# Layer 0's side work kept in emitted order on its engines, gates loaded a group ahead, and v's transposes moved between two groups' items

## The chip, the cores and the metric

One core of one Trainium2 chip. The metric is the device time of one execution in microseconds (us), as the median of several runs of the same program; a smaller number is better. The five engines that work here are TensorE (PE), VectorE (DVE), ScalarE (ACT), GpSimd (POOL) and SyncE (SP, which only issues DMAs in this kernel). Each takes its instructions in one fixed order, and an instruction that waits holds up all that stand behind it on its engine.

## The reference

Two layers of a bidirectional encoder over 512 tokens with 16 learned meta tokens ahead of them (528 rows, width 2048). Layer 0 is grouped-query softmax attention (16 query heads, 8 key/value heads of 128), layer 1 gated linear attention. The change touches layer 0 alone:

```python
y = rmsnorm(h, pre_norm[0])
proj = y @ w_in                                    # q 2048, k 1024, v 1024, gate 2048
q, k, v, gate = jnp.split(proj, [...], axis=-1)
q = apply_axial_rope(rmsnorm(q, q_norm), ...)      # per head of 128
k = apply_axial_rope(rmsnorm(k, k_norm), ...)
o = softmax(q @ k.T * 128 ** -0.5) @ v             # two query heads share one k and v
y = (o * silu(gate)) @ w_out
h = h + rmsnorm(y, post_norm[0])
```

## The kernel before, in words

All matmuls are fp32, done as three products of halves: an activation tile `src` is split into a high part (a cast on ACT, L131) and a rest (a subtraction on DVE, L132), a weight tile likewise (`whi`, `wlo`), and `hi*hi + lo*hi + hi*lo` is summed in PSUM. The normalised input lies as `uh` and `ul` for the whole layer.

**The first part (about 121 to 291 us).** The projections for gates 3 to 12 and for v of seven groups are made two tiles at a time by `seven` (L216), which forms sums of weight quarters on DVE (L233), runs seven products on PE (L240 to L242), copies or adds them up (`y`, ACT L270 and the like, DVE L249), and stores the tiles to DRAM as `g_d` (POOL queue, L569). Beside it runs `first_group` (L524), which normalises and rotates k, q, q of group 0: a square on ACT (L528), sums over the partitions on PE (`ssq`, L536), scale and shift on DVE (L538), `rotate` (L310: four DMAs qs<-qw on POOL's queue, then three multiplies and adds on POOL, L314 to L316), the inverse root on ACT, and the multiply qw*sq on DVE (L543).

**The groups (about 291 to 775 us).** One group per key/value head, some 60.5 us each. In the stretch of group g, PE runs three projections for group g+1 (`project`, L158: k, q, q; tiles `pp`) as its bulk, and between their matmuls stand those of group g's attention: nine items, one each 3.3 us. An item is `softmax`: scores s on PE (L682 to L684), the maximum on DVE (mx, L687), the exponential on ACT (pn, L690; its row sum is inverted on DVE, rs, L696); half a slot later `transposed`: four transposes into pT and one into pTm on PE (L702, L704), read by ACT (ph, L706; pmt, L708) and DVE (pl, L707; pmt, L709), and later the product with v (`weighted`). The PSUM tile s has one buffer. The PSUM pool `ps_t` has two, and pT, pTm and the tiles vps and vpm of v's transposes take them in turn.

**The side work of a group.**

- `rope` (L318) of the three projected tiles, each at three delays after the projection: two partition sums ssq (L327) with sq on DVE (L330), then the inverse root on ACT (L135, L136) and the multiply qw*f (DVE, L334).
- `values(g+1)` (L601): the tile vt is loaded from g_d by SP (L606), at 13.0 it is transposed (PE vps, L611, and vpm, L618), and from there vh is made on ACT (L614), vl on DVE (L615), and the small vm (L620 to L622).
- `stored_gates` (L648) for two gates: load gr<-g_d on POOL's queue (L652), gr times rrow on DVE (L656), the sigmoid as three ACT passes (L139 to L141), gs times gr on POOL (L670); then `inverse` (L637), a load of the stored reciprocals r_d into the same gr buffer, `divided` on POOL (L641, L642), the product with the held o_sb (L663), and the store og_d (L664).

**What sets the order.** The program is emitted by a model of time, `Clock` (L39): each PE matmul of a projection advances it by a cost, and generators and delayed functions are emitted when the model reaches their due time (`yield 8.0`, `clk.after(13.0, ...)`). Then the builder's scheduler orders every engine's queue by priority and by when inputs are ready in its own simulation: it may float an instruction whose inputs are ready early ahead of others emitted before it. So the gates of before do not stand where their generator emits them: gr has two buffers, and a gate's load and its multiplies stand as soon as a buffer is free, about one gate each half group, from 292 us on and up to a group ahead of the stretch for which they are due. `tc.high_priority` raises a stretch of emission; `tc.keep_in_program_order`, which the change brings in as `pin`, ties an instruction behind the one emitted before it on its engine, without a wait.

Of the kernel before, what the change touches and what calls it, by code (L numbers as in the profile page):

```python
# [13 lines left out]
AF = mybir.ActivationFunctionType  # L14
ALU = mybir.AluOpType
# [4 lines left out]
P = 128  # L20
D = 2048
KT = D // P
SEQ = 512
META = 16
T = SEQ + META
# [6 lines left out]
KV = 8  # L32
# [50 lines left out]
def hybrid_encoder(  # L83
# [5 lines left out]
    nc = tc.nc  # L89
    V, A, G, PE = nc.vector, nc.scalar, nc.gpsimd, nc.tensor  # L90
    clk = Clock()

    def pool(stack, name, bufs=1, **kw):
        return stack.enter_context(tc.tile_pool(name=name, bufs=bufs, reuse_waits="tile", **kw))
# [8 lines left out]
    og_d = scratch.tile([KT, P, T], F32, name="og_d")  # L103
    h1_d = scratch.tile([4, P, D], F32, name="h1_d")
    g_d = scratch.tile([21, P, T], F32, name="g_d")
    r_d = scratch.tile([KV, 2, T], F32, name="r_d")
# [189 lines left out]
    rrow = c0.tile([P, T], F32, name="rrow")  # L296
    erow = c0.tile([P, T], F32, name="erow")
# [20 lines left out]
    def rope(qw, sq, outs, steps):  # L318
        rotate(qw, wk.tile([P, T], F32, tag="qs", name="qs"))
        sh = wk.tile([P, T], F32R, tag="sh", name="sh", bufs=1)  # L320
        sl = wk.tile([P, T], F32R, tag="sl", name="sl", bufs=1)
        split(sh, sl, sq)
        f = sq

        def sums(a, b):
            ps = ps_p.tile([P, 512], F32, tag="pp", name="ssq")[:, :b - a]
            PE.matmul(ps, ones_r, sh[:, a:b], start=True, stop=False)  # L327
            PE.matmul(ps, ones_r, sl[:, a:b], start=False, stop=True)
            with tc.high_priority(AHEAD):
                V.scalar_tensor_tensor(f[:, a:b], ps, 1.0 / P, erow[:, a:b], op0=ALU.mult, op1=ALU.add)  # L330

        def late():
            rsqrt_inplace(f)
            V.tensor_tensor(qw, qw, f, op=ALU.mult)  # L334
            for hi, lo, a, b in outs:
                split(hi, lo, qw[:, a:b])
        for step, part in zip(steps, HALVES):
            clk.after(step, lambda part=part: sums(*part))
        clk.after(steps[2], late)
# [11 lines left out]
    vt = c0.tile([P, T], F32, name="vt")  # L351
# [50 lines left out]
    for i, (si, off) in enumerate(((0, 0), (1, 0), (1, P))):  # L402
        for j, (a, b) in enumerate(HALVES):
            n = 2 * i + j
            if n < 3:
                ps = ps_p.tile([P, 512], F32, tag="pp", name="pp")
            else:
                ps = ps_g.tile([P, 512], F32, name=f"g{n}")
            ps = ps[:, :b - a]
# [114 lines left out]
    def first_group():  # L524

        for qw, w in zip(qws, (KN, QN, QN)):
            sq = fr.tile([P, T], F32, tag="sq", name="sq")
            A.activation(sq, qw, AF.Square)  # L528
            A.activation(qw, qw, AF.Copy, scale=col(w))
            for a, b in HALVES:  # L530
                parts = fr.tile([P, 2, HALF], F32R, tag="qs", name="shl")
                sh, sl = parts[:, 0], parts[:, 1]
                split(sh, sl, sq[:, a:b])
                yield 5.6
                ps = ps_t.tile([P, 512], F32, tag="t", name="ssq")[:, :HALF]
                PE.matmul(ps, ones_r, sh, start=True, stop=False)  # L536
                PE.matmul(ps, ones_r, sl, start=False, stop=True)
                V.scalar_tensor_tensor(sq[:, a:b], ps, 1.0 / P, erow[:, a:b], op0=ALU.mult, op1=ALU.add)  # L538
                yield 0.2
            rotate(qw, fr.tile([P, T], F32, tag="qs", name="qs"))  # L540
            rsqrt_inplace(sq)
            yield 9.4
            V.tensor_tensor(qw, qw, sq, op=ALU.mult)  # L543
            yield 0.4

    def y_tiles():
        return [yp.tile([P, T], F32, tag=f"y{i}", name=f"y{i}") for i in range(2)]
# [2 lines left out]
    for h in range(3):  # L550
        y = yp.tile([P, T], F32, tag=f"y{h % 2}", name="y")
# [49 lines left out]
    def values(g):  # L601
        vh = wa.tile([P, 4, P], F32R, tag="vh", name="vh")
        vl = wa.tile([P, 4, P], F32R, tag="vl", name="vl")
        vm = vm_bufs[g % 2]
        if g:
            clk.after(4.0, lambda: nc.sync.dma_start(out=vt, in_=g_d[13 + g]))  # L606

        def late():
            ps = ps_t.tile([P, 512], F32, tag="t", name="vps")
            for t in range(4):  # L610
                PE.transpose(ps[:, t * P:(t + 1) * P], vt[:, t * P:(t + 1) * P], ident)  # L611
            for t in range(4):
                pst = ps[:, t * P:(t + 1) * P]
                A.activation(vh[:, t, :], pst, AF.Copy, scale=rcol[:, t:t + 1])  # L614
                V.scalar_tensor_tensor(vl[:, t, :], pst, rcol[:, t:t + 1], vh[:, t, :].bitcast(F32),  # L615
                                       op0=ALU.mult, op1=ALU.subtract)
            pm = ps_t.tile([P, 512], F32, tag="t", name="vpm")[:META, :P]
            PE.transpose(pm, vt[:, SEQ:T], ident)  # L618
            rm = rcol[:META, 4:5]
            A.activation(vm[0:META], pm, AF.Copy, scale=rm)  # L620
            A.activation(vm[64:64 + META], pm, AF.Copy, scale=rm)
            V.scalar_tensor_tensor(vm[32:32 + META], pm, rm, vm[0:META].bitcast(F32),  # L622
                                   op0=ALU.mult, op1=ALU.subtract)
        clk.after(13.0 if g else 2.0, late)
        return vh, vl, vm

    def qkv(g):
        qk, outs = qks[g % 2]
        vv = values(g)
        for i, c in enumerate((2048 + g * P, 2 * g * P, (2 * g + 1) * P)):  # L630
            qw, sq, evac = take(col(KN if i == 0 else QN))
            project(w_in0, c, HALVES, evac)
            rope(qw, sq, outs[i], (4.0, 8.8, 9.8))
        return qk, vv

    def inverse(h, rb):
        nc.gpsimd.dma_start(out=rb, in_=r_d[h // 2, h % 2:h % 2 + 1, :].broadcast_to([P, T]))  # L637

    def divided(gs, rb):
        by = gs[:, :SEQ].rearrange("p (t q) -> p t q", t=4)  # L640
        G.tensor_tensor(by, by, rb[:, :SEQ].rearrange("p (q t) -> p t q", t=4), op=ALU.mult)  # L641
        G.tensor_tensor(gs[:, SEQ:], gs[:, SEQ:], rb[:, SEQ:], op=ALU.mult)  # L642

    def inverses(g, rs, a):
# [2 lines left out]

    def stored_gates(hs, held):  # L648

        grs = [wa.tile([P, T], F32, tag="gr", name="gr") for _ in hs]  # L650
        for gr, h in zip(grs, hs):
            nc.gpsimd.dma_start(out=gr, in_=g_d[h])  # L652
        yield 8.0
        gss = []
        for gr, h in zip(grs, hs):
            V.tensor_tensor(gr, gr, rrow, op=ALU.mult)  # L656
            gss.append(silu(gr))
            inverse(h, gr)
            yield 5.0
        for gr, gs, h in zip(grs, gss, hs):  # L660
            divided(gs, gr)
            og = held[h % 2]
            G.tensor_tensor(og, og, gs, op=ALU.mult)  # L663
            nc.gpsimd.dma_start(out=og_d[h], in_=og)  # L664
            yield 3.0

    def silu(gr):
        gs = wa.tile([P, T], F32, tag="gs", name="gs", bufs=2)
        sigmoid(gs, gr)
        G.tensor_tensor(gs, gs, gr, op=ALU.mult)  # L670
        return gs

    def gate(h, last_k=None):
# [876 lines left out]
```

## Time and profile before

| | us |
|---|---|
| median of 3 runs | 1800.95 (1796.97 to 1801.56) |
| profiled execution, its own time | 1799.52 |
| its span | 1797.5 |
| PE busy | 1746.3 (97%) |
| DVE, ACT, POOL busy | 1141.4, 1005.9, 383.2 |
| first part with `seven` | about 121 to 291 |
| eight groups | about 291 to 775 |

The span is the time from the first to the last instruction that the profiler recorded; 2.0 us of the execution lie around it. Idle time in front of an instruction is put down to what ended it (the "releaser"). An engine that is 97% busy has few gaps, and what a change of order can bring is the gaps that it closes; so the views that list PE's waits come first, and then the rows that show why the releaser was late.

### The profile page before, as it was taken

The numbers are of one execution on the slowest core, as the hardware profiler recorded it, in microseconds if no ns is written. First come the engines' busy times: TensorE is split into PE (matmuls) and PEld (weight loads), VectorE is DVE, ScalarE is ACT, GpSimd is POOL, SyncE is SP. The second block draws the span as 40 slices with busy tenths as digits, with TensorE's granted clock in tenths as the row PEclk, the third lists the DMA queues.
The fourth block names the chain that finished last, engine by engine and source line by source line (L and its number), as shares of the span: only waits on it lengthen the run. The fifth ranks groups of instructions, "written<-read, shape, count | busy, mean of one in ns | idle before, by whom it ended". The sixth has DMA issues, their size and how long they took to land. (4 is left out here: it accounts for less than half of the span.)

```text
span 1797.5 us, 31585 instructions
## 1 busy us (share of the span) xinstructions
PE 1746.3 (97%) x12427; PEld 1636.9 (91%) x12427; DVE 1141.4 (63%) x1791; ACT 1005.9 (56%) x2056; POOL 383.2 (21%) x492
## 2 busy tenths in 40 slices
PE   8999999999998999999999999999999999999998
PEld 8999999988898889999999899988898989888886
DVE  5867776565656556696757866667585765764223
ACT  5634446576666665654447544468685765853221
POOL 3103202544555453242131101110000100000000
PEclk9999999999999999999999999999999999999999
DMA  8444434334333334264485444343242332344333
GB/s 258 140 121 125 125 119 137 96 85 101 106 92 96 94 93 119 86 202 129 129 242 177 119 130 119 95 133 105 79 116 74 110 95 81 100 150 175 94 94 129
DMA packets 272387, 218.80 MB, mean 122 GB/s; under 512 B 13196, under 2 KB 243280, under 8 KB 271712
## 3 DMA queue, kind: packets, MB, share of 16 engines
q1 hardware_dynamic: 253200, 157.41, 30.9%
q0 software_dynamic: 19040, 59.40, 10.5%
q8 instruction: 97, 1.59, 0.4%
q14 instruction: 50, 0.41, 0.1%
HBM read 176.83 MB, written 33.44 MB: 117 GB/s over the span
## 5 line engine op out<-in xcount | busy, mean ns | idle before, releaser
L154 PE MATMUL pp<-uh,whi 128*128 128x264 f32 (+1 forms) x1872 | 585.4, 313 | 0.7 <-POOL whi L383 0.5
L156 PE MATMUL pp<-uh,wlo 128*128 128x264 f32 (+1 forms) x1872 | 576.1, 308 | 1.5 <-DVE wlo L132 1.2
L155 PE MATMUL pp<-ul,whi 128*128 128x264 f32 (+1 forms) x1872 | 575.7, 308 | 0.8 <-DVE ul L445 0.8
L132 DVE TENSOR_TENSOR wlo<-wraw,whi 128x1024 fp32r<-128x1024 f32 (+1 forms) x226 | 276.2, 1223 | 234.4 <-ACT whi L131 230.5
L131 ACT CAST whi<-wraw 128x1024 fp32r<-128x1024 f32 (+1 forms) x226 | 235.4, 1042 | 256.4 <-PE f L1462 83.4
L156 PEld LDWEIGHTS pp<-uh,wlo 128*128 128x128 f32 x1872 | 353.3, 189 | 18.9 <-DVE wlo L132 1.7
L154 PEld LDWEIGHTS pp<-uh,whi 128*128 128x128 f32 x1872 | 353.3, 189 | 17.4 <-POOL whi L383 0.8
L155 PEld LDWEIGHTS pp<-ul,whi 128*128 128x128 f32 x1872 | 353.7, 189 | 14.7 <-DVE ul L445 1.4
L131 ACT CAST whi<-x 128x1024 fp32r<-128x1024 f32 x72 | 75.5, 1049 | 110.0 <-PE pp L241 55.1
L132 DVE TENSOR_TENSOR wlo<-x,whi 128x1024 fp32r<-128x1024 f32 x72 | 89.9, 1254 | 43.5 <-ACT whi L131 43.5
L240 PE MATMUL px<-uh,whi 128*128 128x264 f32 x288 | 82.7, 287 | 1.9 <-ACT whi L131 1.9
L242 PE MATMUL px<-uh,wlo 128*128 128x264 f32 x288 | 82.8, 288 | 0.7 <-DVE wlo L132 0.7
L241 PE MATMUL px<-ul,whi 128*128 128x264 f32 x288 | 82.2, 285 | 0.0
L687 DVE TENSOR_REDUCE mx<-s 128x1 f32<-128x528 f32 (+1 forms) x72 | 50.6, 703 | 39.4 <-PE s L684 38.7
L1462 PE MATMUL f<-whi,ul 128*128 128x512 f32 x192 | 75.6, 394 | 0.0
L1460 PE MATMUL f<-whi,uh 128*128 128x512 f32 x192 | 75.5, 393 | 0.0
L1461 PE MATMUL f<-wlo,uh 128*128 128x512 f32 x192 | 75.3, 392 | 0.0
L690 ACT ACTIVATE pn<-s,mx 128x528 f32<-128x528 f32 (+1 forms) x72 | 50.1, 696 | 40.5 <-DVE mx L687 40.3
L313 POOL DMA_DIRECT2D qs<-qw x96 | 47.8, 504 | 93.4 <-issue 33.6
L707 DVE TENSOR_TENSOR pl<-pT,ph 128x512 fp32r<-128x512 f32 (+1 forms) x80 | 47.6, 595 | 24.1 <-ACT ph L706 23.4
L240 PE MATMUL pp<-t0h,whi 128*128 128x264 f32 x192 | 55.6, 289 | 3.7 <-ACT y L270 3.7
L240 PEld LDWEIGHTS px<-uh,whi 128*128 128x128 f32 x288 | 54.7, 190 | 2.1 <-ACT whi L131 2.1
(488 smaller groups left out, 4433.4 us busy)
## 6 DMA issues: line engine op xcount, KB each, us to landing
wraw<-in_gla_w_in_dram SPq DMA_DIRECT2D x82, 512.0 KB, 4.0
wraw<-in_attn_w_in_dram SPq DMA_DIRECT2D x75, 512.0 KB, 4.4
wraw<-in_gla_w_out_dram SPq DMA_DIRECT2D x32, 512.0 KB, 3.9
wraw<-in_attn_w_out_dram SPq DMA_DIRECT2D x23, 512.0 KB, 4.3
x<-in_attn_w_in_dram SPq DMA_DIRECT2D x19, 512.0 KB, 4.3
x<-in_gla_w_in_dram SPq DMA_DIRECT2D x14, 512.0 KB, 4.6
qs<-qw POOLq DMA_DIRECT2D x96, 66.0 KB, 4.5
g_d<-y POOLq DMA_DIRECT2D x20, 264.0 KB, 2.4
```

The source lines that it names most:

```text
L131: A.copy(hi, src)
L132: V.tensor_tensor(lo, src, hi.bitcast(F32), op=ALU.subtract)
L154: PE.matmul(ps, wh, uh[:, k, a:b], start=first, stop=False)
L155: PE.matmul(ps, wh, ul[:, k, a:b], start=False, stop=False)
L156: PE.matmul(ps, wl, uh[:, k, a:b], start=False, stop=last)
L240: PE.matmul(ps, w[0][:, k], bh[:, k], start=k == 0 and not more, stop=False, skip_group_check=more)
L241: PE.matmul(ps, w[0][:, k], bl[:, k], start=False, stop=False, skip_group_check=more)
L242: PE.matmul(ps, w[1][:, k], bh[:, k], start=False, stop=k == KH - 1, skip_group_check=more)
L687: V.reduce_max(mx, s, axis=AX.XY, negate=True)
L1460: PE.matmul(ps, uh[:, k, ts], wh[:, kk], start=(k == 0), stop=False)
L1461: PE.matmul(ps, uh[:, k, ts], wl[:, kk], start=False, stop=False)
L1462: PE.matmul(ps, ul[:, k, ts], wh[:, kk], start=False, stop=(k == KT - 1))
```

## The change

No instruction of the computation is added or removed. Four things are done:

1. **Pins.** The Square, the scale-and-shift and the multiply of `first_group`, the gate loads, gr*rrow, gs*gr, the load of the reciprocals, `divided`'s first multiply and the load of vt keep their place in emitted order on their engine. `divided`'s 16-wide tail is not pinned.
2. **Gates a group ahead.** The two gate tiles of the next group are loaded at the end of `stored_gates` of this one; the steps of `stored_gates` have new delays, the second gate begins 2.2 after the first instead of 5.0.
3. **v's transposes** for groups 2 to 7 are due at 5.0 instead of 13.0 (group 1 stays at 13.0, group 0 at 2.0), and vt is loaded 1.0 after the transposes that read it last. vt's new index, 14 + g, is the next group's tile, as before.
4. **New delays** in `first_group` and `rope`.

```diff
--- before.py
+++ after.py
@@ -89,6 +89,7 @@
     nc = tc.nc
     V, A, G, PE = nc.vector, nc.scalar, nc.gpsimd, nc.tensor
     clk = Clock()
+    pin = tc.keep_in_program_order
 
     def pool(stack, name, bufs=1, **kw):
         return stack.enter_context(tc.tile_pool(name=name, bufs=bufs, reuse_waits="tile", **kw))
@@ -525,23 +526,23 @@
 
         for qw, w in zip(qws, (KN, QN, QN)):
             sq = fr.tile([P, T], F32, tag="sq", name="sq")
-            A.activation(sq, qw, AF.Square)
+            pin(A.activation(sq, qw, AF.Square))
             A.activation(qw, qw, AF.Copy, scale=col(w))
             for a, b in HALVES:
                 parts = fr.tile([P, 2, HALF], F32R, tag="qs", name="shl")
                 sh, sl = parts[:, 0], parts[:, 1]
                 split(sh, sl, sq[:, a:b])
-                yield 5.6
+                yield 6.0
                 ps = ps_t.tile([P, 512], F32, tag="t", name="ssq")[:, :HALF]
                 PE.matmul(ps, ones_r, sh, start=True, stop=False)
                 PE.matmul(ps, ones_r, sl, start=False, stop=True)
-                V.scalar_tensor_tensor(sq[:, a:b], ps, 1.0 / P, erow[:, a:b], op0=ALU.mult, op1=ALU.add)
-                yield 0.2
+                pin(V.scalar_tensor_tensor(sq[:, a:b], ps, 1.0 / P, erow[:, a:b], op0=ALU.mult, op1=ALU.add))
+                yield 1.0
             rotate(qw, fr.tile([P, T], F32, tag="qs", name="qs"))
             rsqrt_inplace(sq)
-            yield 9.4
-            V.tensor_tensor(qw, qw, sq, op=ALU.mult)
-            yield 0.4
+            yield 13.0
+            pin(V.tensor_tensor(qw, qw, sq, op=ALU.mult))
+            yield 5.0
 
     def y_tiles():
         return [yp.tile([P, T], F32, tag=f"y{i}", name=f"y{i}") for i in range(2)]
@@ -602,8 +603,9 @@
         vh = wa.tile([P, 4, P], F32R, tag="vh", name="vh")
         vl = wa.tile([P, 4, P], F32R, tag="vl", name="vl")
         vm = vm_bufs[g % 2]
-        if g:
-            clk.after(4.0, lambda: nc.sync.dma_start(out=vt, in_=g_d[13 + g]))
+
+        def load():
+            pin(nc.sync.dma_start(out=vt, in_=g_d[14 + g]))
 
         def late():
             ps = ps_t.tile([P, 512], F32, tag="t", name="vps")
@@ -621,7 +623,9 @@
             A.activation(vm[64:64 + META], pm, AF.Copy, scale=rm)
             V.scalar_tensor_tensor(vm[32:32 + META], pm, rm, vm[0:META].bitcast(F32),
                                    op0=ALU.mult, op1=ALU.subtract)
-        clk.after(13.0 if g else 2.0, late)
+            if g < KV - 1:
+                clk.after(1.0, load)
+        clk.after({0: 2.0, 1: 13.0}.get(g, 5.0), late)
         return vh, vl, vm
 
     def qkv(g):
@@ -630,15 +634,15 @@
         for i, c in enumerate((2048 + g * P, 2 * g * P, (2 * g + 1) * P)):
             qw, sq, evac = take(col(KN if i == 0 else QN))
             project(w_in0, c, HALVES, evac)
-            rope(qw, sq, outs[i], (4.0, 8.8, 9.8))
+            rope(qw, sq, outs[i], ((5.0, 9.5, 10.5), (4.6, 9.0, 10.0), (5.0, 9.5, 10.5))[i])
         return qk, vv
 
     def inverse(h, rb):
-        nc.gpsimd.dma_start(out=rb, in_=r_d[h // 2, h % 2:h % 2 + 1, :].broadcast_to([P, T]))
+        pin(nc.gpsimd.dma_start(out=rb, in_=r_d[h // 2, h % 2:h % 2 + 1, :].broadcast_to([P, T])))
 
     def divided(gs, rb):
         by = gs[:, :SEQ].rearrange("p (t q) -> p t q", t=4)
-        G.tensor_tensor(by, by, rb[:, :SEQ].rearrange("p (q t) -> p t q", t=4), op=ALU.mult)
+        pin(G.tensor_tensor(by, by, rb[:, :SEQ].rearrange("p (q t) -> p t q", t=4), op=ALU.mult))
         G.tensor_tensor(gs[:, SEQ:], gs[:, SEQ:], rb[:, SEQ:], op=ALU.mult)
 
     def inverses(g, rs, a):
@@ -647,27 +651,42 @@
 
     def stored_gates(hs, held):
 
+        grs = ready.pop() if ready else load_gates(hs)
+        gss = []
+
+        def begin(i):
+            pin(V.tensor_tensor(grs[i], grs[i], rrow, op=ALU.mult))
+            gss.append(silu(grs[i]))
+
+        def end(i):
+            divided(gss[i], grs[i])
+            og = held[hs[i] % 2]
+            G.tensor_tensor(og, og, gss[i], op=ALU.mult)
+            nc.gpsimd.dma_start(out=og_d[hs[i]], in_=og)
+        yield 7.0
+        for i, (x, y) in enumerate(((2.2, 0.8), (8.0, 0.0))[:len(hs)]):
+            begin(i)
+            yield x
+            inverse(hs[i], grs[i])
+            yield y
+        for i in range(len(hs)):
+            end(i)
+            yield 3.2
+        if hs and hs[-1] < 12:
+            ready.append(load_gates([h for h in (hs[-1] + 1, hs[-1] + 2) if h < 13]))
+
+    ready = []
+
+    def load_gates(hs):
         grs = [wa.tile([P, T], F32, tag="gr", name="gr") for _ in hs]
         for gr, h in zip(grs, hs):
-            nc.gpsimd.dma_start(out=gr, in_=g_d[h])
-        yield 8.0
-        gss = []
-        for gr, h in zip(grs, hs):
-            V.tensor_tensor(gr, gr, rrow, op=ALU.mult)
-            gss.append(silu(gr))
-            inverse(h, gr)
-            yield 5.0
-        for gr, gs, h in zip(grs, gss, hs):
-            divided(gs, gr)
-            og = held[h % 2]
-            G.tensor_tensor(og, og, gs, op=ALU.mult)
-            nc.gpsimd.dma_start(out=og_d[h], in_=og)
-            yield 3.0
+            pin(nc.gpsimd.dma_start(out=gr, in_=g_d[h]))
+        return grs
 
     def silu(gr):
         gs = wa.tile([P, T], F32, tag="gs", name="gs", bufs=2)
         sigmoid(gs, gr)
-        G.tensor_tensor(gs, gs, gr, op=ALU.mult)
+        pin(G.tensor_tensor(gs, gs, gr, op=ALU.mult))
         return gs
 
     def gate(h, last_k=None):
```

How the order on the engines changes, at three places. Line numbers of the changed kernel stand some 1 to 19 above those of before: L314 to L317 are `rotate` (before L313 to L316), L617 is vl, L624 vm's rest, L641 the load of the reciprocals, L645 and L646 `divided`, L658 gr*rrow, L664 and L665 the product with o_sb and its store, L683 the gate load, L689 gs*gr, L706 mx, L715 rs.

**POOL about the start of group 2, before** (qw_97 and qw_98 are the tiles of the two projected q, qw_96 that of k):

```order
L313 DMA qs<-qw_98 32x528 x4
L641 TENSOR_TENSOR gs<-gs,gr 128x512
L642 TENSOR_TENSOR gs<-gs,gr 128x16
L663 TENSOR_TENSOR o_sb<-o_sb,gs 128x528
L652 DMA gr<-g_d 128x528
L664 DMA og_d<-o_sb 128x528
L314 TENSOR_TENSOR qw_98<-qw_98,cos 128x528
L315 TENSOR_TENSOR qs<-qs,sin 128x528
L316 TENSOR_TENSOR qw_98<-qw_98,qs 128x528
L670 TENSOR_TENSOR gs<-gs,gr 128x528
L313 DMA qs<-qw_96 32x528 x4
L314 TENSOR_TENSOR qw_96<-qw_96,cos 128x528
```

**The same place after:**

```order
L683 DMA gr<-g_d 128x528 x2
L314 DMA qs<-qw_98 32x528 x4
L315 TENSOR_TENSOR qw_98<-qw_98,cos 128x528
L316 TENSOR_TENSOR qs<-qs,sin 128x528
L317 TENSOR_TENSOR qw_98<-qw_98,qs 128x528
L689 TENSOR_TENSOR gs<-gs,gr 128x528
L641 DMA gr<-r_d 128x528
L646 TENSOR_TENSOR gs<-gs,gr 128x16
L314 DMA qs<-qw_96 32x528 x2
L689 TENSOR_TENSOR gs<-gs,gr 128x528
L314 DMA qs<-qw_96 32x528 x2
```

Before, each gate's load stands singly, behind `divided` of a gate ahead of it, and amid the rotation of qw_98; after, both gate loads of a group stand together, ahead of that rotation. The tail of the first gate's `divided` (L646, not pinned) stands ahead of the second gate's multiply, and k's four rotation DMAs stand two and two about that multiply.

**DVE at the start of group 2, before** (tile rs is an item's inverse row sum, sq the scale and shift for `rope`):

```order
L687 TENSOR_REDUCE mx<-s 128x1
L696 RECIPROCAL rs<-sm 128x1
L656 TENSOR_TENSOR gr<-gr,rrow 128x528
L330 SCALAR_TENSOR_TENSOR sq<-ssq,erow 128x264
L687 TENSOR_REDUCE mx<-s 128x1
L334 TENSOR_TENSOR qw_98<-qw_98,sq 128x528
L696 RECIPROCAL rs<-sm 128x1
L132 TENSOR_TENSOR wlo<-wraw,whi 128x1024
```

**The same place after:**

```order
L706 TENSOR_REDUCE mx<-s 128x1
L715 RECIPROCAL rs<-sm 128x1
L617 SCALAR_TENSOR_TENSOR vl<-vps,rcol,vh 128x128
L624 SCALAR_TENSOR_TENSOR vm_3268<-vpm,rcol,vm_3268 16x128
L331 SCALAR_TENSOR_TENSOR sq<-ssq,erow 128x264
L617 SCALAR_TENSOR_TENSOR vl<-vps,rcol,vh 128x128
L706 TENSOR_REDUCE mx<-s 128x1
L617 SCALAR_TENSOR_TENSOR vl<-vps,rcol,vh 128x128
L335 TENSOR_TENSOR qw_98<-qw_98,sq 128x528
L715 RECIPROCAL rs<-sm 128x1
L658 TENSOR_TENSOR gr<-gr,rrow 128x528
L617 SCALAR_TENSOR_TENSOR vl<-vps,rcol,vh 128x128
```

Before, a gate's multiply gr*rrow stands between the first item's rs and the second item's mx; after, it stands behind the second item's mx and rs, and four vl and a vm of the next group's v stand about it, the last vl behind it.

**DVE in the first part, around the multiply qw*sq of the tile qw_96 (L543 before, L544 after), before** (wlo are weight rests, wraw and x the sums of weight quarters, y the products' sums, shl the split of the next square):

```order
L249 TENSOR_TENSOR y_1389<-y_1389 128x264
L233 TENSOR_TENSOR x_755<-wraw,x_755 128x1024
L249 TENSOR_TENSOR y_1388<-px,y_1388 128x264
L132 TENSOR_TENSOR wlo<-x_753,whi 128x1024
L543 TENSOR_TENSOR qw_96<-qw_96,sq 128x528
L132 TENSOR_TENSOR wlo<-x_755,whi 128x1024
L233 TENSOR_TENSOR x_755<-x_753,x_755 128x1024
L132 TENSOR_TENSOR shl<-sq,shl 128x264
L132 TENSOR_TENSOR wlo<-wraw,whi 128x1024
```

**The same place after:**

```order
L250 TENSOR_TENSOR y_1389<-y_1389 128x264
L234 TENSOR_TENSOR x_755<-wraw,x_755 128x1024
L250 TENSOR_TENSOR y_1388<-px,y_1388 128x264
L133 TENSOR_TENSOR wlo<-x_753,whi 128x1024
L133 TENSOR_TENSOR wlo<-x_755,whi 128x1024
L234 TENSOR_TENSOR x_755<-x_753,x_755 128x1024
L133 TENSOR_TENSOR wlo<-wraw,whi 128x1024
L250 TENSOR_TENSOR y_1634<-px,y_1634 128x264
L544 TENSOR_TENSOR qw_96<-qw_96,sq 128x528
L133 TENSOR_TENSOR wlo<-wraw,whi 128x1024
L133 TENSOR_TENSOR shl<-sq,shl 128x264
```

The multiply qw*sq stands four instructions later, behind one more add of y and two more rests of weights; the split of the next square's rest follows.

## The prediction

> **What bounds the kernel now.** I read the page first.
>
> ```profile
> span 1797.5 us, 31585 instructions
> ...
> PE 1746.3 (97%) x12427; PEld 1636.9 (91%) x12427; DVE 1141.4 (63%) x1791; ACT 1005.9 (56%) x2056; POOL 383.2 (21%) x492
> ```
>
> TensorE is the bound. The change leaves its work as it is, so it can only close gaps on PE or open new ones; waits of other engines count through PE alone. The profiled execution took 1799.52 us, of which the span is 1797.5. So I list PE's waits in the stretch of the groups (285 to 780 us; the columns are total us, times, longest), and then those of the first part (100 to 295 us):
>
> ```profile
> PE s L682 <- ACT pn L690: 12.8, 6, 3.0
> PE pT L702 <- DVE pl L707: 6.0, 12, 0.7
> PE vps L611 <- DVE pl L707: 4.2, 6, 1.5
> ```
>
> ```profile
> PE pp L240 <- ACT y L270: 3.7, 2, 3.0
> ...
> PE pp L242 <- DVE wlo L132: 1.1, 1, 1.1
> ```
>
> These 27 waits of 27.8 us are all that the change can work on. The six waits at s are the biggest term. s has one buffer, so an item's scores wait until the exponential of the item before has read it. The timeline of group 2's start shows why that is late (columns: start, duration, engine, line; in brackets the wait and its releaser):
>
> ```profile
> 415.58 0.58 POOL L652 DMA_DIRECT2D gr<-g_d  x1
> ...
> 419.14 0.79 DVE L656 TENSOR_TENSOR gr<-gr,rrow 128x528 f32<-128x528 f32 x1 [4.30 <-DMA gr<-g_d]
> ...
> 420.02 0.65 ACT L139 ACTIVATE gs<-gr 128x528 f32<-128x528 f32 x1 [3.60 <-DVE gr L656]
> ...
> 420.19 0.69 DVE L687 TENSOR_REDUCE mx<-s 128x1 f32<-128x528 f32 x1
> ...
> 422.70 0.68 ACT L690 ACTIVATE pn<-s,mx 128x528 f32<-128x528 f32 x1
> ...
> 423.53 0.39 PE L682 MATMUL s<-kh,qh 128*128 128x264 f32 x1 [1.66 <-ACT pn L690]
> ...
> 427.01 0.66 PE L702 MATMUL pT<-ident,pn 128*128 128x128 f32 x4 [0.66 <-DVE pl L707]
> ```
>
> The gate's load is issued at 415.58. DVE stands 4.30 us at the multiply that needs it, with the second item's maximum queued behind. That maximum ends at 420.88, the exponential starts only at 422.70, because the gate's sigmoid has gone onto ACT ahead of it, and PE waits 1.66 us at s. A side step that stands ahead of the attention's own chain thus makes the wait; PE's other two waits inside a group come from the two buffers that pT and v's vps share.
>
> **What a wait costs beyond its row.** Two prices are not in those rows. PE's matmuls start 0.12 us apart when nothing holds them:
>
> ```profile
> 359.90 0.28 PE L155 MATMUL pp<-ul,whi 128*128 128x264 f32 x1
> 360.02 0.28 PE L156 MATMUL pp<-uh,wlo 128*128 128x264 f32 x1
> ...
> 363.31 0.39 PE L682 MATMUL s<-kh,qh 128*128 128x264 f32 x1 [3.00 <-ACT pn L690]
> ```
>
> From 360.02 to 363.31 are 3.29 us, 3.17 more than a step of 0.12, for a wait of 3.00: each wait costs its row and 0.17. And the granted clock falls after the longest waits. In windows of 2 us (columns after the width: PE, PEld, DVE, ACT, POOL, then the clock, the DMA share, GB/s):
>
> ```profile
> 169.00:171.00 2.00, 1.81 (x8) 1.81 (x9) 1.88 (x3) 2.00 (x4) 0.00 (x0) 0.52 0.71 195
> 364.00:366.00 2.00, 2.00 (x11) 2.00 (x10) 1.78 (x3) 1.58 (x6) 0.00 (x1) 0.50 0.00 0
> 366.00:368.00 2.00, 2.00 (x16) 2.00 (x14) 1.91 (x6) 1.21 (x2) 0.00 (x0) 0.74 0.61 168
> ```
>
> After the 3.00 at 363.31 the clock is 0.50 and 0.74 over 4 us, which loses 2 x 0.50 + 2 x 0.26 = 1.5 us; the wait of 3.0 at L240 (it ends at 169) starts with 0.52. I take 1.6 for each of the two. [...]
>
> **The change part by part.**
>
> *Gates loaded a group ahead and pinned.* For groups 2 to 7 the loads stand behind qw_97's rotation, one projection (a third of 60.5, some 20 us) ahead of the multiply; the load above took 419.14 - 415.58 = 3.6 us from issue to the multiply. And the multiply stands behind the second item's mx and rs. So mx waits for PE alone and the exponential follows it.
>
> ```profile
> L656 DVE TENSOR_TENSOR gr<-gr,rrow x13: 687/785/1798, 297.5 to 635.0; 128x528 f32<-128x528 f32 x13
> ...
> L139 ACT ACTIVATE gs<-gr x32: 614/635/654, 298.2 to 1599.7; 128x528 f32<-128x528 f32 x16, 128x512 f32<-128x512 f32 x16
> ```
>
> The six waits at s go: 12.8. Only group 1's two loads stand behind the rotation of qw_98, a short way ahead of their multiply; I leave 1.0 us for that group, between 0 (they land in time) and the 3.0 of the longest wait at s.
>
> *v's transposes at 5.0.* There no item of the new group has a pT yet, so they take both buffers without a wait, and the first pT of a group no longer takes its buffer in the turn of an item that pl still reads. Five of six vps waits go (group 1's place is unchanged): 5/6 x 4.2 = 3.5. Of the twelve at pT, five stand at a group's second item and are like 427.01's 0.66, by my count of the timeline: 3.3 goes. The seven at the ends of groups, 6.0 - 3.3 = 2.7, stay, since no edit is near them. New is that the first pTm wants the buffer that vl reads, and the last vl stands behind rs and gr*rrow on DVE:
>
> ```profile
> L614 ACT ACTIVATE vh<-vps,rcol x32: 356/368/376, 293.3 to 679.1; 128x128 fp32r<-128x128 f32 x32
> L615 DVE SCALAR_TENSOR_TENSOR vl<-vps,rcol,vh x32: 341/351/354, 294.3 to 679.5; 128x128 fp32r<-128x128 f32 x32
> ```
>
> ```profile
> 412.00:430.00 18.00, 15.68 (x128) 15.25 (x127) 8.29 (x15) 10.46 (x26) 10.28 (x10) 1.00 0.35 93
> ```
>
> The work queued ahead of that pTm on DVE is gr*rrow and one vl, 0.785 + 0.351 = 1.1 us, and I charge 0.7 us, between 0 and 3.0, as such waits at pT show now (0.66), for six groups: 4.2. The load of vt lies after the reads of the tile before and has 40 us to land, so it costs nothing; SP's weight loads behind it are not delayed by one transfer.
>
> *More ACT work at the group's start.* In 412 to 430 ACT is busy 10.46 of 18 us, with one gate's sigmoid. After, a second sigmoid comes in (3 x 0.635 = 1.9) and v's casts (4 x 0.368, and two small ones that I take alike: 2.2): 14.6 of 18 us. ACT keeps up, but a cast ph can stand behind a sigmoid pass: 0.4 us for each of six groups, 2.4, between 0 and one sigmoid, 1.9 each.
>
> *The first part.* PE waits for y (L270), which stands behind a Square on ACT that waits for DVE's multiply, which waits for POOL's rotation:
>
> ```profile
> 165.14 1.31 POOL L316 TENSOR_TENSOR qw<-qw,qs 128x528 f32<-128x528 f32 x1
> ...
> 166.48 0.71 DVE L543 TENSOR_TENSOR qw<-qw,sq 128x528 f32<-128x528 f32 x1 [3.88 <-POOL qw L316]
> ...
> 167.28 0.64 ACT L528 ACTIVATE sq<-qw 128x528 f32<-128x528 f32 x1 [5.66 <-DVE qw L543]
> ```
>
> With 13.0 in place of 9.4 the multiply stands 3.6 us later in the queue, against a wait of 3.88, and the Square follows it, so both engines are released at about the time that they come there. 3.7 and 1.1 go, 4.8. The whole chain of three tiles grows by 3 x (2 x 1.2 + 3.6 + 4.6) = 32 us, but it has room: its first rotation ends at 165.14 + 1.31, so it began about 20 us before, and with 3 x 32 = 96 us it ends near 245, where `seven` goes on to 291. A store behind POOL's rotation (L569) has no reader near.
>
> *The sum.* Gone: 12.8 + 3.5 + 3.3 + 4.8 = 24.4; the steps of 6 + 5 + 5 + 3 = 19 waits, 19 x 0.17 = 3.2; the clock 2 x 1.6 = 3.2; together 30.8. New: 1.0 + 4.2 + 2.4 = 7.6. The gain is 23.2, so 1799.5 - 23.2 = 1776.3 for an execution like the profiled one; the median is 1.4 above that one, so 1778. Behind 780 us nothing takes the gain back: PE's work there follows its own queue.
>
> **The rivals.**
>
> *B: gr*rrow collides with POOL.* Its row above has 687 ns at least and 1798 at most, so something adds 1.1 us to it at times. The multiply would now stand beside POOL's rotation in every group, with the last vl behind it and pTm behind that: 6 x 1.1 = 6.6 us less gain, 1778 + 6.6 = 1785. For it speaks the 1798, against it the median of 785. [...]
>
> *C: the waits move to pT and pTm.* If ACT's vh come late, the last vl and vm come late, and the shared buffers with them: 2.5 us at pTm and 0.7 at pT for each of six groups, with two steps of 0.17, 6 x 3.54 = 21.2 in place of the 6.6 that I charge: 14.6 less, 1793. For it speaks that pT already waits twelve times for that pool of buffers; against it that v's work now starts when nothing else uses them.
>
> *D: slower.* ACT at the start of a group is the place. Exponentials of the new items queue behind two sigmoids and v's casts; if ACT falls behind by a slot of 3.3 us, PE waits again in each of six groups and the clock halves. A wait of x costs x + 0.17 + 1.6. What goes without the 6.6 charged leaves 1778 - 6.6 = 1771, so it is slower than 1801 from 30 / 6 = 5.0, that is x = 3.2; at 4.0 it is 1771 + 6 x 5.8 = 1806. Against it: 14.6 of 18 us leaves ACT 3.4 us free, and the two sigmoids cannot stand ahead of one exponential together, as they are 2.2 apart and pinned.
>
> *E: nothing comes of it.* The pins hold other things back by what they free: 1801.
>
> **How the numbers follow.** The forecast has 0.57, B 0.12, C 0.15, D 0.09, E 0.07. A difference of 0.3%, 5.4 us, is about what a measurement of this kernel can tell from none. Forecast, B and nearly all of C lie beyond it on the fast side: 0.83; E and the rest of C within it: 0.08; D: 0.09. The range begins where nothing new is charged and the ends of the groups are freed too (1771 - 1.0 - 2.7 - 7 x 0.17 = 1766), and ends at C with 3.2 in place of 2.5 at pTm, 1797; D, E and the tails outside leave less than 0.2.
>
> **What would show it.** Right: in 285 to 780 us the row of s waiting for pn is gone or below 3 us, DVE's wait for gr<-g_d is left in one group, pT's total is about 3 to 6, and in the first part L240 waits less than 1 us; the windows show no clock below 0.9 in the groups. B shows as gr*rrow at a median over 1.5 us; C as a row of pTm or pT above 15 us; D as waits at s or pT over 3 us with a clock of 0.5 behind each. The prediction is wrong if PE's waits in the groups sum to more than 15 us, or if they fall below it and the time does not follow.

## The result, and the profile after

The changed kernel takes 1776.76 us (median of 4 runs, 1776.39 to 1778.32) against 1798.96 us before (4 runs): a ratio of 0.9878, 95% interval 0.9860 to 0.9896. The prediction said 1778, range 1766 to 1797. The page of the profiled execution:

```profile
span 1776.4 us, 31587 instructions
...
PE 1737.5 (98%) x12427; PEld 1635.0 (92%) x12427; DVE 1153.0 (65%) x1791; ACT 1000.4 (56%) x2056; POOL 386.9 (22%) x492
```

PE has the same 12427 matmuls and a span that is 21.1 us shorter. Where the time went can be read from the matmul that all groups share, the scores s. The tile's row of before, then of after (ahead of the form stand the least, the median and the longest duration in ns, then the first and the last start in us):

```profile
L682 PE MATMUL s<-kh,qh x144: 280/284/422, 293.1 to 755.3; 128*128 128x264 f32 x128, 128*32 128x264 f32 x16
```

```profile
L701 PE MATMUL s<-kh,qh x144: 280/284/389, 290.4 to 738.5; 128*128 128x264 f32 x128, 128*32 128x264 f32 x16
```

The first scores come 2.7 us earlier, the stretch from the first to the last is 448.1 in place of 462.2 us, 14.1 less, and the rest of the span, 1037.9 for 1042.2, is 4.3 less. Nothing behind takes the gain back. PE's order at the end of the last group is not the same in the two kernels: after, 23 more matmuls stand between the first and the last scores (3536 for 3513). A stretch with like work ends at the last matmul of the output projection `po` (3801 matmuls after, 3802 before): 481.7 in place of 497.7 us, 16.0 less, and behind it 1004.3 in place of 1006.7, 2.4 less. Of these 2.4 us, 1.7 are a fall of the granted clock at 1046 us in the trace of before, which the trace of after does not have; the change touches nothing there.

PE's waits in the groups (280 to 770 us) after the change, and the one that is left in the first part (100 to 295):

```profile
PE pT L721 <- DVE pl L726: 12.4, 7, 2.5
PE ssq L328 <- ACT sh L132: 1.9, 7, 0.7
PE pTm L723 <- DVE vl L617: 1.0, 1, 1.0
PE pTm L723 <- DVE pl L726: 0.6, 1, 0.6
PE sums L749 <- DVE pl L726: 0.2, 1, 0.2
```

```profile
PE pp L243 <- DVE wlo L133: 2.1, 1, 2.1
```

The six waits at s are gone, and so is the row of vps. But pT, which had 6.0 us in twelve waits, has 12.4 in seven. Six of them, 10.7 us, stand at one place in groups 1 to 6, behind the transposes of the meta item (the fifth of the nine); the seventh, 1.7 us, stands at the second item of the last group. The timeline of one of the six, and then the seventh:

```profile
488.77 1.57 POOL L645 TENSOR_TENSOR gs<-gs,gr 128x512 f32<-128x512 f32 x1
488.90 2.53 DVE L133 TENSOR_TENSOR wlo<-wraw,whi 128x1024 fp32r<-128x1024 f32 x1 [0.55 <-ACT whi L132]
490.42 2.19 POOL L664 TENSOR_TENSOR o_sb<-o_sb,gs 128x528 f32<-128x528 f32 x1
...
496.33 1.30 POOL L664 TENSOR_TENSOR o_sb<-o_sb,gs 128x528 f32<-128x528 f32 x1
496.55 1.65 DVE L335 TENSOR_TENSOR qw<-qw,sq 128x528 f32<-128x528 f32 x1
498.22 0.23 DVE L726 TENSOR_TENSOR pl<-pT,ph 128x64 fp32r<-128x64 f32 x1
...
498.60 0.63 PE L721 MATMUL pT<-ident,pn 128*128 128x128 f32 x4 [2.21 <-DVE pl L726]
```

```profile
708.92 0.63 PE L721 MATMUL pT<-ident,pn 128*128 128x128 f32 x4 [1.71 <-DVE pl L726]
```

A weight rest that takes 1.23 us elsewhere takes 2.53, because POOL's `divided` began 0.13 us before it; POOL's next multiply then takes 2.19 for the 1.30 of its later instance. The multiply qw*f takes 1.65 in place of 0.71 beside the next product with o_sb. The meta item's pl stands behind them, and PE waits 2.21 us for it. POOL's instruction ends at 488.77 + 1.57 = 490.34 and the weight rest 1.1 us later, so 1.1 of the 1.23 us that it takes elsewhere lie behind POOL's instruction. The prediction's rival B was a collision with POOL too, but at another instruction. The lines of the weight rests in the groups, before and after (behind the bar busy us and mean ns, then DVE's idle time ahead of them and what ended it), show the change over all of them:

```profile
L132 DVE TENSOR_TENSOR wlo<-wraw,whi 128x1024 fp32r<-128x1024 f32 x47 | 58.3, 1241 | 18.9 <-ACT whi L131 15.3 <-PE ssq L328 3.1
```

```profile
L133 DVE TENSOR_TENSOR wlo<-wraw,whi 128x1024 fp32r<-128x1024 f32 x47 | 67.8, 1443 | 23.6 <-ACT whi L132 23.4
```

So one theory, P, is that POOL's multiplies of the stored gates, which now run in one stretch of each group, make the new pT waits. Its rivals are V, that v's moved transposes make them by the turns of the two buffers, and A, that ACT's work at this place does.

### The profile page after: what moved, and what is told of

The parts are those of the page before. It is cut to its first block, busy times and chain, and to the rows that moved or that the text cites. A ratio compares the mean times of both kernels' runs of the same rounds, so it can differ in the third digit from the quotient of the medians.

```text
span 1776.4 us, 31587 instructions
## 1 busy us (share of the span) xinstructions
PE 1737.5 (98%) x12427; PEld 1635.0 (92%) x12427; DVE 1153.0 (65%) x1791; ACT 1000.4 (56%) x2056; POOL 386.9 (22%) x492
## 4 chain that ended last, share of the span: by engine, by line
PE 77%; issue 7%; DVE 7%; ACT 5%; DMA 2%; POOL 2%; SPq 0%; DVEq 0%; POOLq 0%; ACTq 0%
PE pp L155 12%; PE pp L157 12%; PE pp L156 12%; PE pp L241 3%; PE pp L242 3%; PE pp L243 3%; PE f L1481 2%; PE f L1479 2%; PE f L1480 2%; PE px L243 2%; PE px L241 2%; PE px L242 2%; DVE wlo L133 2%; ACT whi L132 2%; PE pT L721 1%
## 5 line engine op out<-in xcount | busy, mean ns | idle before, releaser
L133 DVE TENSOR_TENSOR wlo<-wraw,whi 128x1024 fp32r<-128x1024 f32 (+1 forms) x226 | 287.9, 1274 | 238.4 <-ACT whi L132 237.9
L706 DVE TENSOR_REDUCE mx<-s 128x1 f32<-128x528 f32 (+1 forms) x72 | 50.8, 706 | 52.8 <-PE s L703 52.3
L243 PE MATMUL px<-uh,wlo 128*128 128x264 f32 x288 | 82.0, 285 | 0.8 <-DVE wlo L133 0.8
L241 PE MATMUL px<-uh,whi 128*128 128x264 f32 x288 | 82.2, 285 | 0.4 <-ACT whi L132 0.4
L314 POOL DMA_DIRECT2D qs<-qw x96 | 48.0, 506 | 95.1 <-ACT sq L308 72.9
L243 PE MATMUL pp<-t0h,wlo 128*128 128x264 f32 x192 | 54.4, 283 | 2.1 <-DVE wlo L133 2.1
L243 PEld LDWEIGHTS px<-uh,wlo 128*128 128x128 f32 x288 | 54.1, 188 | 1.0 <-DVE wlo L133 1.0
```

What stands on the lines that cost most here:

```text
L133: V.tensor_tensor(lo, src, hi.bitcast(F32), op=ALU.subtract)
L241: PE.matmul(ps, w[0][:, k], bh[:, k], start=k == 0 and not more, stop=False, skip_group_check=more)
L243: PE.matmul(ps, w[1][:, k], bh[:, k], start=False, stop=k == KH - 1, skip_group_check=more)
L706: V.reduce_max(mx, s, axis=AX.XY, negate=True)
```

## The experiments

Times are medians of device time; each ratio is to the kernel before as it ran beside it on the same chip (1797.14, 1796.07 and 1796.72 us on the three chips), with its 95% interval.

**The gates alone.** v's transposes, the load of vt and `first_group` as before:

```diff
-        clk.after({0: 2.0, 1: 13.0}.get(g, 5.0), late)
+        clk.after(13.0 if g else 2.0, late)
...
+        if g:
+            clk.after(4.0, lambda: nc.sync.dma_start(out=vt, in_=g_d[13 + g]))
```

> Only the gates' edits (loads a group ahead, pins on the gate steps, the new delays of stored_gates and rope); v's transposes and the first group as before. Theory P (POOL's products, divided and o_sb, now run in one stretch and block DVE there, which makes the new 2 us waits at the pT behind the meta item): the s waits of 12.8 us and one clock drop of 1.6 go, the new pT waits come, about +9.7, vps stays at about 4: 1799 - 15.4 + 9.7 = 1793, pT row above 12 us, wlo up to 2.5 us. Rival V (the new pT wait comes from v's transposes, which shift the turns of the two PSUM buffers): no new pT wait here, 1799 - 15.4 = 1784.

1779.73 us, ratio 0.9898 (0.9882 to 0.9914). PE's first row of waits in the groups:

```profile
PE pT L718 <- DVE pl L723: 7.8, 7, 2.4
```

The new pT waits are there without v's move, so V falls as their main cause. They are smaller than in the whole change (P had expected more than 12), and, against both expectations, vps has no wait left although v's transposes stand where they stood; the time is below both, 1793 and 1784. The gates' edits, `rope`'s new delays among them, take the vps waits of before away too.

**v's move alone.** The opposite edit: only `values` is changed.

> Only v's transposes at 5.0 and vt's load behind the transposes before; gates and first group as before. Theory P: vps (3.5) and the first pT of a group (3.3) go with their steps of 0.17, the s waits stay: 1799 - 8.5 = 1790, no pT wait over 1 us. Rival V: the pT waits of about 2 us come here, 1799 - 8.5 + 9.7 = 1800.

1808.91 us, ratio 1.0069 (1.0054 to 1.0084): slower, which neither theory had. PE's waits, and the start of group 2:

```profile
PE pTm L708 <- DVE vl L617: 12.1, 5, 2.5
PE pT L706 <- DVE vm L624: 10.3, 5, 3.3
```

```profile
415.01 0.58 POOL L656 DMA_DIRECT2D gr<-g_d  x1
...
419.26 1.46 DVE L660 TENSOR_TENSOR gr<-gr,rrow 128x528 f32<-128x528 f32 x1 [4.88 <-DMA gr<-g_d]
...
422.36 0.34 DVE L624 SCALAR_TENSOR_TENSOR vm<-vpm,rcol,vm 16x128 fp32r<-16x128 f32 x1 [0.26 <-ACT vm L623]
...
422.75 0.66 PE L706 MATMUL pT<-ident,pn 128*128 128x128 f32 x4 [3.15 <-DVE vm L624]
...
426.07 0.45 PE L708 MATMUL pTm<-ident,pn 128*96 128x128 f32 x1 [2.54 <-DVE vl L617]
```

The gate's multiply, still floated, waits 4.88 us for its load on DVE; now not only mx but also the vl and vm that hold both PSUM buffers come behind that wait, and PE waits 3.15 and 2.54 us within 3.3. The granted clock after them:

```profile
424.00:426.00 2.00, 0.00 (x0) 0.00 (x0) 1.57 (x5) 2.00 (x6) 0.00 (x0) 0.50 0.00 0
426.00:428.00 2.00, 1.93 (x9) 1.94 (x10) 1.42 (x3) 2.00 (x7) 0.00 (x0) 0.50 0.00 0
```

This is rival D's price, PE's wait and the halved clock, but the engine that was late first is DVE, by the wait for a load. (D's slot of 3.3 us is one of the emission's model of time; in the trace of before, the scores of one group stand 4.5 to 8.4 us apart.)

**The first group alone.** Only `first_group` with its pins and delays:

> Only the first group's pins and delays. The two waits at L240 and the clock drop of the first part go and a wait of about 2 us on wlo comes: 1799 - 4.8 = 1794, the groups unchanged with s waits of about 13 us. Rival: the first part's end only moves into a later wait, 1799.

1791.18 us, ratio 0.9964 (0.9951 to 0.9978). The L240 waits are gone, L243 waits 1.8 us for wlo in the first part, and the groups keep the waits of before, with less at s in this execution:

```profile
PE s L683 <- ACT pn L691: 8.3, 5, 3.3
```

The medians differ by 6.0 us, so the rival falls. Not all of the 6.0 is the part's own: in the trace its first scores come 3.6 us earlier than before (289.5 for 293.1), and the rest is gained behind them, where the edit itself does nothing. Over the nine traces that have this edit with its pins, the first scores come at 287.4 to 290.4, against 293.1 to 293.3 in the three with the first group as before: 2.7 to 5.9 us.

**No pins.** The whole change, with

```diff
-    pin = tc.keep_in_program_order
+    pin = lambda i: i
```

> The whole change with its new emission order and delays, but without the pins. Theory (the pins hold the gate steps back): the scheduler floats the gate multiply ahead of the attention's maximum again, s waits of 8 to 13 us are back: 1787 to 1793. Rival (the emission order alone does it): 1777.

1807.61 us, ratio 1.0063 (1.0044 to 1.0082), slower by 31 us than the changed kernel by the medians. PE's waits, and DVE's for the gate's load:

```profile
PE pT L721 <- DVE vm L624: 15.5, 5, 4.3
PE pTm L723 <- DVE vl L617: 12.3, 6, 2.5
```

```profile
DVE gr L658 <- DMA gr<-g_d: 28.1, 9, 6.0
```

This is the picture of v's move alone. The theory was right that the pins keep the gate steps back, but not on the place: the wait stands at pT and pTm, ahead of the next s, and it costs more than the waits at s did.

**One pin.** As the last, with the pin of gr*rrow on DVE put back and no other:

```diff
+            tc.keep_in_program_order(V.tensor_tensor(grs[i], grs[i], rrow, op=ALU.mult))
```

> The whole change with one pin alone, that of gr*rrow on DVE; the other pins are gone. If this pin carries what the pins bring (without any it was 1808, with waits of 28 us at pT and pTm): 1776 to 1782. Rival (the loads of the gates and gs*gr on POOL have to be pinned as well, else the loads float ahead of or behind the rotations and the multiply waits): 1790 to 1800.

1777.83 us, ratio 0.9900 (0.9886 to 0.9913). This one pin carries nearly all that the pins bring; what is left to the others is seen in the first part, where L241 waits for y again:

```profile
PE pp L243 <- DVE wlo L133: 2.3, 1, 2.3
PE pp L241 <- ACT y L271: 2.2, 1, 2.2
```

**Without POOL's products.** `divided` and the product with o_sb are left out:

```diff
         def end(i):
-            divided(gss[i], grs[i])
             og = held[hs[i] % 2]
-            G.tensor_tensor(og, og, gss[i], op=ALU.mult)
```

> The change, with divided and the product with o_sb left out of the stored gates (POOL's three multiplies per gate; the output lacks these factors for heads 0 to 12). Theory P (these multiplies block DVE's two-input instructions beside them and so make the item behind the meta item late): DVE's wlo is back below 1.7 us, the pT row of 12.4 us falls to about 3, the time to about 1767. Rival A (ACT, with two sigmoids and v's casts in the same stretch, makes it late): pT stays above 10, 1777.

1764.78 us, ratio 0.9821 (0.9806 to 0.9837), about 10 us below the whole change by the ratios (0.9878). In the traces, the stretch from the first scores to the last matmul of `po` is 9.2 us shorter (472.5 for 481.7). The pT waits, two of the seven, and the weight rests in the groups:

```profile
PE pT L719 <- DVE pl L724: 5.4, 7, 1.7
```

```profile
419.85 0.63 PE L719 MATMUL pT<-ident,pn 128*128 128x128 f32 x4 [0.83 <-DVE pl L724]
...
697.26 0.63 PE L719 MATMUL pT<-ident,pn 128*128 128x128 f32 x4 [1.73 <-DVE pl L724]
```

```profile
L133 DVE TENSOR_TENSOR wlo<-wraw,whi x47: 1215/1226/1229, 295.7 to 730.2; 128x1024 fp32r<-128x1024 f32 x47
```

No weight rest takes over 1.229 us any more, and the pT row falls by 7.0. The 3 us that P expected are not reached, but none of the 5.4 that are left stands behind the meta item: that place went from 10.7 us to nothing. Six waits of 0.5 to 0.8 us are new, at the third item of groups 1 to 6, and the one in the last group is as it was (1.73 for 1.71), so that one does not come from the products.

**Without the sigmoid.** One ACT pass for the three of each stored gate:

```diff
-            gss.append(silu(grs[i]))
+            gss.append(silu(grs[i], False))
...
-        sigmoid(gs, gr)
+        if full:
+            sigmoid(gs, gr)
+        else:
+            A.activation(gs, gr, AF.Exp, scale=-1.0)
```

> The change, with one ACT pass in place of the three of a stored gate's sigmoid (so the gate factor of heads 0 to 12 is another function). Rival A: ACT is relieved by 1.3 us for each gate, the pT row falls below 6, about 1770. Theory P: the pT row stays at about 12, wlo up to 2.5 us, 1777.

1774.38 us, ratio 0.9873 (0.9855 to 0.9891), not to be told from the whole change (0.9878). The pT row:

```profile
PE pT L724 <- DVE pl L729: 11.1, 7, 2.6
```

A falls: 26 ACT passes less, and the wait stays.

**The products later.** 14.0 in place of 8.0:

```diff
-        for i, (x, y) in enumerate(((2.2, 0.8), (8.0, 0.0))[:len(hs)]):
+        for i, (x, y) in enumerate(((2.2, 0.8), (14.0, 0.0))[:len(hs)]):
```

> The change, with the delay ahead of the stored gates' end 14.0 in place of 8.0, which puts divided and the product with o_sb behind the second q's rotation on POOL instead of the first k's. Theory P: the products meet the meta item no more, its pT waits fall from 12.4 to 3 to 6 us in all, 1768 to 1771. Rival (they slow DVE's weight rests wherever they stand, and the next item waits instead): 1777.

1774.40 us, ratio 0.9874 (0.9860 to 0.9889): no gain that can be told. Both were half right. The pT waits vanish but for 0.2 us, and a new row comes at the end of the group (PE's waits, then the timeline of one):

```profile
PE ssq L328 <- ACT sh L132: 10.3, 7, 2.0
...
PE pT L721 <- DVE pl L726: 0.2, 1, 0.2
```

```profile
394.06 1.32 POOL L664 TENSOR_TENSOR o_sb<-o_sb,gs 128x528 f32<-128x528 f32 x1
394.18 1.77 DVE L335 TENSOR_TENSOR qw<-qw,sq 128x528 f32<-128x528 f32 x1 [0.47 <-POOL gs L646]
...
399.28 0.39 PE L328 MATMUL ssq<-sh,ones_r 128*128 128x264 f32 x1 [1.98 <-ACT sh L132]
```

The product meets the second q's multiply instead, and ssq comes late behind that.

**Gates and first group, without v's move.**

> The gates' and the first group's edits together, v's transposes and vt's load as before. By the runs of the parts alone: 1779.7 - 6.0 = 1773.8, so v's move costs about 3 us in the whole change, pT row at about 8. Rival (v's move saves the vps waits of 4.2 us and the first part does not add up): 1780.

1771.41 us, ratio 0.9860 (0.9841 to 0.9880), pT row 6.2 us.

The changed kernel and the two of the next paragraphs then ran together on one chip, for smaller differences.

> The changed kernel again, on the same chip as the next two for comparison: 0.986 to 0.990 of before, near 1776, the pT row at 12 us in all.

1775.30 us, ratio 0.9882 (0.9868 to 0.9895), pT row 10.6.

> The gates' and the first group's edits without v's move, beside the whole change on the same chip. If v's move costs where the gates are already put right (its casts and rests come onto DVE and ACT ahead of the meta item): 3 to 6 us below the whole change, pT row 6 to 8 us. Rival (the difference seen was the chip's): within 2 us of the whole.

1774.04 us, ratio 0.9883 (0.9866 to 0.9901), pT row 6.8. In two traces out of two v's move adds 4 to 6 us to the pT row, but the times beside each other are the same: whether v's move costs a little, once the gates are right, stays open. It brings nothing that can be measured.

**The product on DVE.** As the last, with the product done on DVE one step later:

```diff
         def end(i):
             divided(gss[i], grs[i])
+
+        def put(i):
             og = held[hs[i] % 2]
-            G.tensor_tensor(og, og, gss[i], op=ALU.mult)
+            pin(V.tensor_tensor(og, og, gss[i], op=ALU.mult))
             nc.gpsimd.dma_start(out=og_d[hs[i]], in_=og)
...
+        for i in range(len(hs)):
+            put(i)
+            yield 0.6
```

> As the kernel before this one, with the product with o_sb done on DVE, one step later, in place of POOL (13 multiplies of about 0.7 us there instead of 1.3 to 2.2 on POOL). Theory P: fewer of DVE's instructions are blocked, wlo's longest below 2 us, the pT row from 6 to 3 or 4: 2 to 4 us below gates_first. Rival (DVE's own added work, 2 x 0.7 us in one place, makes the item there late by as much): no gain.

1769.41 us, ratio 0.9852 (0.9838 to 0.9865): 4.6 us below the kernel beside it and 5.9 below the whole change by the medians; its interval ends just below those of both, and overlaps with that of the earlier run of gates and first group. PE's waits in the groups:

```profile
PE sums L751 <- DVE pl L728: 3.3, 1, 3.3
PE pT L723 <- DVE pl L728: 2.1, 2, 1.4
```

P's prices hold here in size: the pT row goes from 6.8 to 2.1, with DVE doing more work, not less. Behind the meta item one wait of 0.65 us is left of six with 6.4; the 1.4 is that of the last group. A part of P's expectation failed: the longest weight rest is still 2.359 us. What went is the collision with qw*f, whose longest is 0.709 in this kernel and 1.679 in gates_first. One wait of 3.3 us in the last group is new. By its median it is the fastest kernel of the study that leaves nothing out; that it is faster than gates and first group without this edit is not clear of the noise.

## Why the prediction was right, point by point

- **PE's waits are all that the change can work on**: right in the main; the 27.8 us leave out nine waits of 1.8 us at ssq and vpm. The chain at s was read rightly (load, DVE's multiply, mx, pn); all 12.8 us went, and DVE's wait for gr<-g_d fell from 28.9 to 1.1 us, in one group.
- **Group 1's late load, 1.0**: right. gr*rrow waits 1.1 us for its load there, the last vl stands behind it, and PE waits 1.0 at pTm for that vl.
- **The first part, 4.8 and a clock drop**: the two waits at L240 went and the clock is 1.00 there, but a wait of 2.1 at L243 is new. Of the 4.8 + 3 x 0.17 + 1.6 = 6.9 us reckoned, 2.7 came in this trace, and no more than 5.9 in any other.
- **v's transposes, 3.5 + 3.3**: the mechanism was wrong. The waits at vps went, and so did four of the five at the second item's pT (that of the last group went from 0.6 to 1.7). But the gates' edits alone take them away, and v's move alone makes the kernel 0.7% slower. I had put them down to the turns of the buffers. For group 0, where v's transposes stand at 13.0 in every kernel, the runs show that the floated multiply, with the gate's steps behind it, makes the wait: vps waits 0.5 us without pins and not at all with the one pin. For the other groups the runs do not part the multiply from `rope`'s new delays.
- **"The seven at the ends of groups, 6.0 - 3.3 = 2.7, stay, since no edit is near them"**: this step failed. They stand behind the meta item in the middle of a group (one of before at 329.60, 36.5 us after the group's first scores at 293.1), and an edit is near: the products of both gates now run there one behind the other. Six of the seven places measure 10.7 in place of 2.5 us; that of group 0, where no stored gate runs, has none.
- **pTm 4.2 and ACT 2.4**: over-reckoned. pTm has 1.6 in all, of which 1.0 is group 1's late load, and a run with 26 ACT passes less is no faster. The charge of 6.6, of which 0.6 came, and the 12.4 - 2.7 = 9.7 that came unforeseen at pT cancel in large part. That is luck.
- **B**: gr*rrow never takes over 0.708 us after; it collides with nothing. In the trace of before, its 1.80 us stand at 454.36, 0.09 us behind the start of POOL's product with o_sb (454.27, 1.32 us long). After, the collisions are at wlo (2.53 for 1.23 us) and qw*f (1.65 for 0.71), and cost about 7 us of waits at pT and some 10 us of time, as the run without the products shows. **C and D** did not come in the whole change, but their waits did, with a clock of 0.50, in the two kernels without the gate's pin.
- By its own test, PE's waits in the groups under 15 us, the prediction fails by a little: the five rows make 16.1. That the time still came out at 1777 rests on the s waits, which were foreseen, and beside them on terms that cancel. The forecast's sum and the two traces, place by place (us gained; 23.9 is what was to go in the groups, with one fall of the clock and the steps of 16 waits, and 7.6 what was charged as new):

| | forecast | measured |
|---|---|---|
| to the first scores | 6.9 | 2.7 |
| from there to the last matmul of `po` | 23.9 - 7.6 = 16.3 | 16.0 |
| behind it | 0 | 2.4 |
| in all | 23.2 | 21.1 |

The rows of the groups fell by 8.7 us (from 24.8, with ssq's and vpm's 1.8 of before, to 16.1); with 16 fewer steps of 0.17 and the clock's 1.7 that is 13.1 of the 16.0 us. The rest is not settled. Steps of 0.2 to 0.3 us between matmuls, which no row of waits carries, number 150 in this stretch of before (those at the halved clock among them) and 119 of after.

## What to carry to other kernels

One side instruction that a scheduler floats ahead of its due place, and that then waits for a load, holds up all behind it on its engine (DVE stood 4.88 us at gr*rrow in v's move alone, and the vm behind it made PE wait 3.15 us); look for a wait on a DMA on a side engine first, and try one pin there before a dozen. An edit that gives work an earlier place can be worth less than nothing until that wait is gone, as v's move was (1808.91 us alone, ratio 1.0069). And when side work is gathered into one stretch, look at what runs beside it on other engines: the gathered products of POOL made single long instructions of DVE twice as long (2.53 for 1.23 us, 1.65 for 0.71).

## What the runs showed of the hardware

After some waits the granted clock fell to half: the two last windows of this section lose 2 x 0.34 + 2 x 0.50 = 1.7 us of full clock, and in v's move alone it is 0.50 in all three windows from 424 to 430. It does not go by the length of one wait alone. In before a wait of 2.84 us that ends at 546.08 left it at 1.00; in the kernel with the product on DVE it fell to 0.50 after a wait of 1.92 us:

```profile
546.00:548.00 2.00, 1.92 (x15) 1.92 (x16) 1.16 (x2) 2.00 (x6) 0.79 (x1) 1.00 0.04 8
```

```profile
179.21 0.39 PE L243 MATMUL pp<-t0h,wlo 128*128 128x264 f32 x1 [1.92 <-DVE wlo L133]
```

Two executions of the same kernel can differ. The changed kernel's wait of 2.46 us at 615.92 left the clock at 1.00; in its second trace it fell to 0.63 and 0.52 in the two windows after the wait of 2.36 us at that place, which ends at 613.27:

```profile
614.00:616.00 2.00, 2.00 (x14) 2.00 (x13) 1.97 (x4) 1.22 (x3) 1.17 (x3) 0.63 0.80 237
616.00:618.00 2.00, 2.00 (x11) 2.00 (x11) 0.47 (x3) 0.85 (x4) 1.22 (x1) 0.52 0.02 4
```

The three falls of before begin in these windows:

```profile
169.00:170.00 1.00, 0.81 (x3) 0.81 (x4) 1.00 (x1) 1.00 (x4) 0.00 (x0) 0.54 0.37 98
363.00:364.00 1.00, 0.69 (x4) 0.70 (x5) 0.16 (x1) 1.00 (x3) 1.00 (x1) 0.82 0.00 0
1046.00:1047.00 1.00, 1.00 (x8) 1.00 (x7) 1.00 (x2) 1.00 (x2) 0.00 (x0) 0.65 0.00 0
```

Ahead of the first, PE waits 3.00 us at L240 (to 169.19); ahead of the second, 3.00 us at s (to 363.31); ahead of the third, 1.92 and then 0.75 us (to 1043.92 and 1045.18). So waits of 1.9 to 3.0 us stand ahead of falls, while those of 2.46 and 2.84 us brought none. What decides was not shown, and no run was made to test it. The windows behind the wait of 1.92 us in the kernel with the product on DVE:

```profile
179.00:181.00 2.00, 1.79 (x9) 1.79 (x10) 2.00 (x2) 0.00 (x0) 1.32 (x1) 0.66 0.29 76
181.00:183.00 2.00, 2.00 (x11) 2.00 (x11) 2.00 (x4) 0.00 (x0) 0.00 (x0) 0.50 0.63 186
```

So a sum should hold a price for each wait of 2 to 3 us, as a chance, and not only for the two longest.
